# A decoder step on one core: page numbers read later, the first norm's squares added by VectorE, a longer burst of products of ones

## The chip, the cores and the metric

The kernel runs on one core of a Trainium2 chip. The metric is the device time of one execution in microseconds. Shown are the median of three runs and one profiled execution. TensorE multiplies, VectorE and ScalarE prepare and evacuate operands, GpSimd does small side work, and SP (SyncE) issues nearly all loads. ScalarE's queue issues three of them.

## What is computed

One inference step of a two-layer decoder for 256 prompt rows and 8 sample rows (264 columns in all, T), model width 1024. The part that the change touches is the start of layer 0:

```python
def moba_gmlp_mixer(x, pos, past_kv, norm_g, w_in, ...):
    h = rmsnorm(x, norm_g)                       # mean of squares over 1024 features, per row
    z = h @ w_in                                 # 1024 x 2560
    q, k, v, bu, bv = split(z)
    q, k = rope_partial(q, pos), rope_partial(k, pos)
    k_all, v_all = cached pages (page_table) + new k, v   # sample rows only
    a = moba_attention(q, k_all, v_all, pos)     # 8 heads
    b = spatial_gating(gelu(bu), layer_norm(gelu(bv)))
    return x + concat(a, b) @ w_out
```

A ConvFFN (width 2816), a second layer with stick-breaking attention and a pooling mixer, another ConvFFN and a final norm follow. Each of the 8 sample rows has two cached pages of keys and two of values in each layer, found through a page table of 16 numbers.

## The kernel before

Activations lie transposed: features on the 128 partitions, 264 columns in the free dimension, 8 feature tiles. Weights come in blocks of 128x128, in the order in which TensorE uses them. Every fp32 weight block and every operand is split into a high and a low part (`wh`, `wl`; `xg_h`, `xg_l`), ScalarE making the high part and VectorE the low part by a subtraction. Each block then takes three products (high x high, high x low, low x high) of 264 columns each. Eight blocks are one split tile; `wsp` holds four such tiles.

The first norm is applied late: the products of layer 0 use x times the gain, and the factor R (one over the root of the mean square) is multiplied in when a result leaves PSUM. So the squares and the sum for R run beside the first products. `norm0` (line 655) issues the product with a matrix of ones that sums over partitions, then Ln and Exp on ScalarE give R, and three VectorE operations make the rope tables times R. Results that are ready before R (`held`) wait in PSUM.

The first 16 weight blocks arrive with the input in six pieces (`xw`, lines 346 to 352), then come four loads of eight blocks (`raw` 2 to 5, 0.5 MB each) and, from `raw` 6 on, loads of sixteen blocks (1 MB). Calls with `keep_in_program_order` (`late` is one for loads) hold the written order on their engine; the other instructions are ordered by a planner. In the loop `run`, work is hung on block counts: `blk(n, f)` calls f after n of the 160 blocks of layer 0's input projection. TensorE's order is held there (`fixed[0]`), so a product that waits holds all behind it. `page_regs` (line 337) has SP read page numbers from the loaded page table into registers; K and V pages are loaded by `drip_of`, two pages a call. `square` and `sqw` do not exist before; `Norm.add` squares on ScalarE and adds on GpSimd. `WARM` products of ones (128x256, bf16) start TensorE before the first operand is there.

Order of the places that matter: `norm0` at block 30, K pages from block 24 to 80, V pages from 80 to 136, scores S of the prompt from block 82 (`s_qk`), sample scores (`sm_score`) at 131, sample values (`pv_l`, lines 491 to 502) at 157 and 159.

Of the kernel before, what the change touches and what calls it, by code (L numbers as in the profile page):

```python
# [13 lines left out]
AF = mybir.ActivationFunctionType  # L14
ALU = mybir.AluOpType
# [19 lines left out]

MMB = 4
KQ = 5
WARM = 12
YD = ((0, 1), (1, 3), (3, 5), (5, 7), (7, 8))

NEG = -1e30
# [161 lines left out]
def tile_decoder_step(ctx: ExitStack, tc: tile.TileContext, a):  # L203
    nc = tc.nc
    v, s, g = nc.vector, nc.scalar, nc.gpsimd
# [25 lines left out]
    def f4(name, shape=(P, 4, T), dt=F32):  # L231
        return up.tile(list(shape), dt, tag="u", name=name)

    def mv(name):
        return [f4(f"{name}_{x}", dt=F32R) for x in "hl"]
# [4 lines left out]
    def at(name):  # L240
        return psa.tile([P, 512], F32, tag="at", name=name)
# [13 lines left out]
    def vec(n):  # L255
        o, w = _VEC[n]
        return VEC[:, o:o + w]
# [15 lines left out]
    def late(dst, src):  # L273
        tc.keep_in_program_order(nc.sync.dma_start(dst, src))

    def wtiles(tt):
        return [wsp.tile([P, 8 * P], F32R, tag=f"w{x}", name=f"w{x}{tt}") for x in "hl"]

    def raw(ci):
        if ci not in raws:  # L280
            n = _CHUNKS[ci] * P
            r = f4(f"raw{ci}", (P, n)) if ci < C8 else rawp.tile([P, n], F32, tag="raw", name=f"raw{ci}")
            o = (coff[ci] - 16) * P * P
            raws[ci] = r
            late(r, a["w"][o:o + P * n].rearrange("(p f) -> p f", p=P))
        return raws[ci]
# [49 lines left out]
    regs = []  # L336

    def page_regs(n):
        for i in range(len(regs), len(regs) + n):
            regs.append(nc.sync.value_load(PT[0:1, i:i + 1], min_val=0, max_val=NPHYS - 1))  # L340
# [3 lines left out]
    first, o = [], 0  # L344
    for i in range(len(_FIRST)):
        g_, w_, x_ = _first_cols(i)
        n = g_ + w_ + x_
# [4 lines left out]
        if i == 4:  # L352
            raw(2)
    tc.keep_in_program_order(s.dma_start(PT, a["pt"]))
    for c in (3, 4):
        raw(c)
        page_regs(2)
    late(CS, a["rope"].rearrange("p (c t) -> p c t", c=2))
    raw(5)
    page_regs(4)  # L360
    late(CST, a["cst"])
    raw(6)
    page_regs(4)
    late(VEC, a["vec"])
    page_regs(4)
    GAIN = first[0][0]
    xin = [x[:, i, :] for _, _, x in first for i in range(x.shape[1])]
    tc.keep_in_program_order(s.preload_act_table_set("natural_log_exp_and_others"))
# [2 lines left out]
    pw = at("warm")  # L371
    for i in range(WARM):
        tc.keep_in_program_order(pe.matmul(pw[:, :256], warm[:, :P], warm, start=i == 0, stop=i == WARM - 1))

# [9 lines left out]
    def operand_tile(dst, m, src, gain, pin=False):  # L384
        h, l = dst[0][:, m % 4, :], dst[1][:, m % 4, :]
        i = s.activation(h, src, AF.Copy, scale=gain)  # L386
        j = v.scalar_tensor_tensor(l, src, gain, h.bitcast(F32), ALU.mult, ALU.subtract)  # L387
        if pin:
            tc.keep_in_program_order(i)
            tc.keep_in_program_order(j)  # L390

    class Norm:
# [8 lines left out]
        def add(self, m, src=None):  # L401
            q = sm.tile([P, T], F32, tag="sq", name=f"sq_{self.name}{m}")
            i = s.activation(q, X[:, m, :] if src is None else src, AF.Square)
            if src is not None:
                tc.keep_in_program_order(i)
            if m == KD - 1 and self.two:
                self.last.append(q)
            elif self.acc is None:
                self.acc = q
            elif m == (0 if self.seeded else 1):  # L410
                n = sm.tile([P, T], F32, tag="acc", name=f"acc_{self.name}", bufs=2)
                g.tensor_tensor(n, self.acc, q, ALU.add)
                self.acc = n
            else:
                g.tensor_tensor(self.acc, self.acc, q, ALU.add)
# [36 lines left out]
    def page_list(cache, name):  # L452

        tiles, todo = [], []

        def load(i):
            if i % NPG == 0:
                tiles.append(f4(f"{name}_{i}", (P, NPG, 512)))
            late(tiles[i // NPG][:, i % NPG, :], cache[bass.ds(regs[i], 1), :, :].rearrange("o p f -> (o p) f"))

        return tiles, [lambda i=i: load(i) for i in range(NS * NPG)]

    def drip_of(todo, n):
        def f():
            for _ in range(min(n, len(todo))):
                todo.pop(0)()
        return f
# [122 lines left out]
    def residual(gain, name, operand=True, R=None, plain=False):  # L590
        xg = [mv(f"xg_{name}{i}") for i in range(2)] if operand else None
        nrm = Norm(name, not operand)

        def evac(m, o):
            m = m[1]
            if R is not None and not plain:
                z = sm.tile([P, T], F32, tag="rz", name=f"z_{name}{m}", bufs=4)
                v.tensor_tensor(z, o, R, ALU.mult)
                o = z
            v.tensor_tensor(X[:, m, :], X[:, m, :], o, ALU.add)  # L600
            if operand:
                operand_tile(xg[m // 4], m, X[:, m, :], gain[:, m:m + 1])
            nrm.add(m)
            if not operand:
                s.activation(X[:, m, :], X[:, m, :], AF.Copy, scale=gain[:, m:m + 1])
        return xg, nrm, evac
# [7 lines left out]

    xg = [mv(f"xg_0{i}") for i in range(2)]
    nrm = Norm("n0", True)
    for tt in range(2):
        splits[tt] = wtiles(tt)

    def part(i, eng):  # L620

        (b, e), _ = _FIRST[i]
        h, l = [w[:, (b % 8) * P:(b % 8) * P + (e - b) * P] for w in splits[b // 8]]
        src = first[i][1]
        tc.keep_in_program_order(s.activation(h, src, AF.Copy) if eng is s else v.tensor_copy(h, src))
        return lambda: tc.keep_in_program_order(v.tensor_tensor(l, src, h.bitcast(F32), ALU.subtract))

    def whole(tt):
        h, l = splits[tt] = wtiles(tt)
        ci = chunk_of[tt]  # L630
        o = (tt * 8 - coff[ci]) * P
        src = raws[ci][:, o:o + 8 * P]
        tc.keep_in_program_order(s.activation(h, src, AF.Copy))
        tc.keep_in_program_order(v.tensor_tensor(l, src, h.bitcast(F32), ALU.subtract))
# [4 lines left out]
    for m in range(1, 5):  # L639
        part(m, s)()  # L640
        operand_tile(xg[m // 4], m, xin[m], GAIN[:, m:m + 1], pin=True)
        if m != 2:
            nrm.add((m - 1) // 2 if m < 4 else 2, xin[(m - 1) // 2 if m < 4 else 2])
    whole(2)
    for m in range(5, KD):
        operand_tile(xg[m // 4], m, xin[m], GAIN[:, m:m + 1], pin=True)
    for m in range(3, KD):
        nrm.add(m, xin[m])
        if m == 4:
            whole(3)  # L650
        elif m == 6:
            whole(4)
    rope = f4("rope")
    R0, held = [], []

# [43 lines left out]
    ktiles, kload = page_list(a["kt0"], "K0")  # L699
    vtiles, vload = page_list(a["vp0"], "V0")  # L700
# [164 lines left out]
    blk = lambda b, f, *x: hk.at(b / 8 - 1, f, *x)  # L865
# [8 lines left out]
        late(X[:, m:m + 2, :], a["x"].rearrange("p (m t) -> p m t", t=T)[:, m:m + 2, :])  # L874

    for n in range(8):
        blk(24 + 8 * n, drip_of(kload, 2))
        blk(80 + 8 * n, drip_of(vload, 2))
    for m in range(0, KD, 2):
        blk(120 + 4 * m, late_x, m)  # L880
    blk(30, norm0)
    blk(40, masks)
    blk(44, gm_first)
    blk(72, sm_q)
# [39 lines left out]
    xg, nrm, evac = residual(vec("f0"), "f0")  # L924
# [5 lines left out]
    ktiles, kload = page_list(a["kt1"], "K1")  # L930
    vtiles, vload = page_list(a["vp1"], "V1")
# [143 lines left out]
    blk = lambda b, f, *x: hk.at(b / 8 - 1, f, *x)  # L1075
# [28 lines left out]
    xg, nrm, evac = residual(vec("f1"), "f1")  # L1104
# [4 lines left out]
    _, nrm, evac = residual(vec("fin"), "fin", operand=False, R=R, plain=True)  # L1109
# [13 lines left out]
    for i, (m, e) in enumerate(YD):  # L1123
        x = X[:, m:e, :]
# [71 lines left out]
```

## Time and profile before

| | us |
|---|---|
| median of three runs | 602.36 (602.09 to 602.79) |
| the profiled execution | 603.04 |
| its span, first to last instruction | 601.1 |
| TensorE busy | 589.8 (98% of the span) |
| VectorE busy | 425.0 (71%) |
| ScalarE busy | 341.5 (57%) |
| GpSimd busy | 45.5 (8%) |

The profile's page gives busy time and the chain of work that ended last; the views of the trace give, for any stretch, each engine's instructions in order of time, who waited for whom, and the stretch's sums (its start and end, its length, each engine's busy time with the number of instructions, the granted TensorE clock as a share of full speed, the busy share of the load engines and what they moved). "L300" is line 300 of the kernel. PE is TensorE, PEld its weight loads, DVE VectorE, ACT ScalarE, POOL GpSimd, SPq and ACTq the queues that issue loads. Durations of neighbouring instructions on one engine overlap a little, so where a queue is full, the distance from one start to the next is what an instruction costs.

### The profile page before, as it was taken

The page shows a single profiled execution, that of the slowest core. Times are in us where ns is not written, and L with a number is a line of the kernel's source. Part 1 is how long each engine was busy: PE and PEld are TensorE (multiplying, and loading weights), DVE is VectorE, ACT ScalarE, POOL GpSimd, SP SyncE. Part 2 cuts the span into 40 slices and gives each one's busy share as a digit, 9 for nine tenths or more (in the row PEclk, how much of TensorE's full clock was granted, in tenths as well). Part 3 has the DMA queues.
Part 4 walks back from the last instruction along what each step waited for, and adds up shares of the span by engine and source line. Part 5 has one row for each costly group of instructions (what it writes and reads, how often), then busy time and mean ns, then how long its engine had stood idle before and what let it go on. Part 6 is the DMA issues. An engine that isn't in the chain of part 4 may idle for free.

```text
span 601.1 us, 12276 instructions
## 1 busy us (share of the span) xinstructions
PE 589.8 (98%) x4900; PEld 571.1 (95%) x4900; DVE 425.0 (71%) x745; ACT 341.5 (57%) x601; POOL 45.5 (8%) x63
## 2 busy tenths in 40 slices
PE   8999999999999999999999999999999999999994
PEld 7988879999999999999999879999999999999994
DVE  7799665877877778576659676688777787755432
ACT  7657854675555655454453456657565555555441
POOL 4100002400000000001110000130000000002110
PEclk9999999999999999999999999999999999999998
DMA  8998835455454545796467763554645445464502
GB/s 316 355 396 309 294 146 198 156 196 177 174 204 154 203 166 185 261 372 215 154 246 257 270 196 109 172 207 145 210 150 201 177 176 203 152 214 163 189 1 72
DMA packets 28090, 122.39 MB, mean 204 GB/s; under 512 B 3330, under 2 KB 5250, under 8 KB 16642
## 3 DMA queue, kind: packets, MB, share of 16 engines
q1 hardware_dynamic: 27200, 120.42, 56.0%
q10 hardware_dynamic: 834, 1.20, 0.6%
q8 instruction: 38, 0.62, 0.4%
q14 instruction: 18, 0.15, 0.1%
HBM read 117.65 MB, written 3.96 MB: 202 GB/s over the span
## 4 chain that ended last, share of the span: by engine, by line
PE 92%; DVE 3%; DMA 2%; SPq 1%; issue 1%; ACT 0%; ACTq 0%; DVEq 0%
PE mm L215 85%; DMA raw<-in_w 1%; PE pv_l L215 1%; PE sc L215 1%; DVE wl L300 1%; PE pav L215 1%; PE pt L218 1%; DMA PT<-in_pt 1%; PE S L215 1%; SPq L340 1%; PE Z L215 1%; PE pf L215 0%; DVE X L1125 0%; DVE rz_q L689 0%; PE pm L215 0%
## 5 line engine op out<-in xcount | busy, mean ns | idle before, releaser
L300 DVE TENSOR_TENSOR wl<-raw,wh 128x1024 fp32r<-128x1024 f32 x179 | 220.0, 1230 | 113.8 <-ACT wh L299 113.3
L299 ACT ACTIVATE wh<-raw 128x1024 fp32r<-128x1024 f32 x179 | 189.7, 1062 | 193.6 <-PE mm L215 181.6
L215 PE MATMUL mm<-xg_f_h,wh 128*128 128x264 f32 x704 | 200.3, 284 | 0.1
L215 PE MATMUL mm<-xg_f_l,wh 128*128 128x264 f32 x704 | 200.0, 284 | 0.0
L215 PE MATMUL mm<-xg_f_h,wl 128*128 128x264 f32 x704 | 198.6, 282 | 0.0
L215 PEld LDWEIGHTS mm<-xg_f_h,wh 128*128 128x128 f32 x704 | 132.2, 188 | 0.3 <-DVE wk L582 0.3
L215 PEld LDWEIGHTS mm<-xg_f_l,wh 128*128 128x128 f32 x704 | 132.2, 188 | 0.0
L215 PEld LDWEIGHTS mm<-xg_f_h,wl 128*128 128x128 f32 x704 | 132.2, 188 | 0.0
L215 PE MATMUL mm<-a_h,wh 128*128 128x264 f32 x352 | 99.9, 284 | 0.0
L215 PE MATMUL mm<-a_l,wh 128*128 128x264 f32 x352 | 99.8, 284 | 0.0
L215 PE MATMUL mm<-a_h,wl 128*128 128x264 f32 x352 | 99.3, 282 | 0.0
L215 PEld LDWEIGHTS mm<-a_l,wh 128*128 128x128 f32 x352 | 66.1, 188 | 0.0
L215 PEld LDWEIGHTS mm<-a_h,wh 128*128 128x128 f32 x352 | 66.1, 188 | 0.0
L215 PEld LDWEIGHTS mm<-a_h,wl 128*128 128x128 f32 x352 | 66.1, 188 | 0.0
L215 PE MATMUL mm<-xg_h,wh 128*128 128x264 f32 x160 | 48.2, 301 | 0.9 <-ACT xg_h L386 0.9
L215 PE MATMUL mm<-xg_l,wh 128*128 128x264 f32 x160 | 46.2, 289 | 0.0
L215 PE MATMUL mm<-xg_h,wl 128*128 128x264 f32 x160 | 46.1, 288 | 0.1
L215 PE MATMUL mm<-xg_n_h,wh 128*128 128x264 f32 x128 | 38.6, 302 | 0.0
L215 PE MATMUL mm<-xg_n_l,wh 128*128 128x264 f32 x128 | 36.3, 283 | 0.0
L215 PE MATMUL mm<-xg_n_h,wl 128*128 128x264 f32 x128 | 36.2, 283 | 0.0
L215 PEld LDWEIGHTS mm<-xg_h,wh 128*128 128x128 f32 x160 | 30.8, 192 | 4.1 <-issue 2.7
L215 PEld LDWEIGHTS mm<-xg_l,wh 128*128 128x128 f32 x160 | 30.8, 192 | 0.3 <-DVE xg_l L387 0.2
(245 smaller groups left out, 845.3 us busy)
## 6 DMA issues: line engine op xcount, KB each, us to landing
raw<-in_w SPq DMA_DIRECT2D x89, 1024.0 KB, 4.8
K<-in_kt SPq DMA_DIRECT2D x32, 256.0 KB, 6.8
V<-in_vp SPq DMA_DIRECT2D x32, 256.0 KB, 5.5
raw<-in_w SPq DMA_DIRECT2D x4, 512.0 KB, 5.9
X<-in_x SPq DMA_DIRECT2D x4, 264.0 KB, 7.1
xw<-in_xw SPq DMA_DIRECT2D x2, 388.0 KB, 5.2
out_k<-k SPq DMA_DIRECT2D x1, 528.0 KB
out_v<-v SPq DMA_DIRECT2D x1, 528.0 KB, 4.4
```

The lines of the kernel that those rows point to most:

```text
L215: return self.keep(nc.tensor.matmul(*x, **k))
L218: return self.keep(nc.tensor.transpose(*x, **k))
L299: s.activation(h, src, AF.Copy)
L300: v.tensor_tensor(l, src, h.bitcast(F32), ALU.subtract)
L340: regs.append(nc.sync.value_load(PT[0:1, i:i + 1], min_val=0, max_val=NPHYS - 1))
```

## The change

Four things change.

1. SP reads no page number among its first loads; the loads 3 to 6, the rope table, the constants and the vectors are issued one behind the other. Each page number is read when the first K load that needs it is issued.
2. K pages are issued from block 40 to 96 instead of 24 to 80, V pages from block 104 to 146 (every six blocks) instead of 80 to 136 (every eight).
3. The squares of the first norm go to two wide tiles of four feature tiles each. VectorE adds them in three instructions of 1056, 528 and 264 columns, held in order behind its part of split 4. GpSimd adds nothing here any more. The product of ones has one operand instead of two and stands at block 34 instead of 30. The squares of tiles 3 to 7 come behind split 3 on ScalarE.
4. Eighteen products of ones instead of twelve start TensorE.

```diff
-WARM = 12
+WARM = 18
@@
     tc.keep_in_program_order(s.dma_start(PT, a["pt"]))
-    for c in (3, 4):
+    for c in (3, 4, 5):
         raw(c)
-        page_regs(2)
     late(CS, a["rope"].rearrange("p (c t) -> p c t", c=2))
-    raw(5)
-    page_regs(4)
+    raw(6)
     late(CST, a["cst"])
-    raw(6)
-    page_regs(4)
     late(VEC, a["vec"])
-    page_regs(4)
@@
         def load(i):
+            if i >= len(regs):
+                page_regs(1)
             if i % NPG == 0:
@@
     nrm = Norm("n0", True)
+    sqw = [f4(f"sqw{i}") for i in range(2)]
+
+    def square(m):
+        tc.keep_in_program_order(s.activation(sqw[m // 4][:, m % 4, :], xin[m], AF.Square))
+
@@
         operand_tile(xg[m // 4], m, xin[m], GAIN[:, m:m + 1], pin=True)
-        if m != 2:
-            nrm.add((m - 1) // 2 if m < 4 else 2, xin[(m - 1) // 2 if m < 4 else 2])
+        if m < 4:
+            square(m - 1)
     whole(2)
     for m in range(5, KD):
         operand_tile(xg[m // 4], m, xin[m], GAIN[:, m:m + 1], pin=True)
+    whole(3)
     for m in range(3, KD):
-        nrm.add(m, xin[m])
-        if m == 4:
-            whole(3)
-        elif m == 6:
-            whole(4)
+        square(m)
+    whole(4)
+    add = lambda o, x, y: tc.keep_in_program_order(v.tensor_tensor(o, x, y, ALU.add))
+    add(sqw[0], sqw[0], sqw[1])
+    add(sqw[0][:, 0:2, :], sqw[0][:, 0:2, :], sqw[0][:, 2:4, :])
+    add(sqw[0][:, 0, :], sqw[0][:, 0, :], sqw[0][:, 1, :])
+    nrm.acc = sqw[0][:, 0, :]
@@
-        blk(24 + 8 * n, drip_of(kload, 2))
-        blk(80 + 8 * n, drip_of(vload, 2))
+        blk(40 + 8 * n, drip_of(kload, 2))
+        blk(104 + 6 * n, drip_of(vload, 2))
@@
-    blk(30, norm0)
+    blk(34, norm0)
```

## Rows read from the trace of the kernel before

**Rows 1.** The page, part 4: the chain that ended last, by engine.

```profile
PE 92%; DVE 3%; DMA 2%; SPq 1%; issue 1%; ACT 0%; ACTq 0%; DVEq 0%
```

**Rows 2.** Stretches: PE, PEld, DVE, ACT, POOL busy (instructions), clock, load share, GB/s.

```profile
0.00:5.00 5.00, 2.93 (x13) 1.79 (x13) 0.92 (x5) 2.04 (x4) 2.14 (x12) 1.00 0.61 213
4.00:8.60 4.60, 3.79 (x15) 3.50 (x16) 3.78 (x9) 4.12 (x10) 0.22 (x1) 1.00 1.03 416
8.60:18.00 9.40, 9.35 (x77) 9.13 (x76) 9.33 (x10) 7.64 (x15) 5.80 (x6) 1.00 0.96 339
...
23.00:39.40 16.40, 15.23 (x126) 14.90 (x125) 16.37 (x41) 11.60 (x15) 0.00 (x0) 1.00 1.04 403
100.00:200.00 100.00, 100.00 (x828) 100.00 (x827) 78.16 (x132) 61.21 (x108) 7.17 (x8) 1.00 0.51 180
```

**Rows 3.** TensorE's waits, 0 to 60 us: total us, times, longest.

```profile
PE S L215 <- DVE k L695: 1.2, 1, 1.2
```

**Rows 4.** The chain in order of time: start us, us, what.

```profile
1.66 4.86 DMA PT<-in_pt
...
12.93 7.80 DMA raw<-in_w
...
39.41 0.93 PE S L215 x8
```

**Rows 5.** ScalarE in order of time: start, us, line, operation, count, [idle before].

```profile
9.45 1.05 ACT L633 ACTIVATE wh<-raw 128x1024 fp32r<-128x1024 f32 x1
10.40 1.32 ACT L386 ACTIVATE xg_h<-xw,xw 128x264 fp32r<-128x264 f32 x3
11.62 0.73 ACT L403 ACTIVATE sq_n<-xw 128x264 f32<-128x264 f32 x2
...
20.83 1.06 ACT L299 ACTIVATE wh<-raw 128x1024 fp32r<-128x1024 f32 x1 [4.02 <-DMA raw<-in_w]
21.80 0.46 ACT L438 ACTIVATE R_n<-ns_n,epst 128x264 f32<-128x264 f32 x1
22.29 0.42 ACT L439 ACTIVATE R_n<-R_n 128x264 f32<-128x264 f32 x1
```

**Rows 6.** VectorE in order of time, with GpSimd's first add.

```profile
6.68 0.69 DVE L626 TENSOR_TENSOR wl<-xw,wh 128x512 fp32r<-128x512 f32 x1 [0.33 <-ACT wh L625]
...
8.38 1.02 POOL L412 TENSOR_TENSOR acc_n<-sq_n,sq_n 128x264 f32<-128x264 f32 x1 [5.71 <-ACT sq_n L403]
...
8.86 1.09 DVE L626 TENSOR_TENSOR wl<-xw,wh 128x512 fp32r<-128x512 f32 x1
...
21.93 1.22 DVE L300 TENSOR_TENSOR wl<-raw,wh 128x1024 fp32r<-128x1024 f32 x1 [3.18 <-ACT wh L299]
23.07 0.43 DVE L659 TENSOR_TENSOR rope<-ropecs,R_n 128x264 f32<-128x264 f32 x1
...
55.91 1.24 DVE L824 TENSOR_TENSOR bv<-bv,mu 128x1056 f32<-128x1056 f32 x1
```

**Rows 7.** TensorE's products in order of time.

```profile
1.20 2.74 PE L215 MATMUL warm<-warm 128*128 128x256 bf16 x12 [1.20 <-DVE warm L370]
4.81 0.59 PE L215 MATMUL mm<-xg_h,wh 128*128 128x264 f32 x1 [0.87 <-ACT xg_h L386]
...
8.48 0.32 PE L215 MATMUL mm<-xg_h,wl 128*128 128x264 f32 x1
...
18.04 0.61 PE L215 MATMUL ns_n<-acc_n,ones 128*128 128x264 f32 x2
18.48 0.61 PE L215 MATMUL ns_n<-sq_n,ones 128*128 128x264 f32 x2
```

**Rows 8.** The page table: who touches it, duration min/median/max ns, first and last start.

```profile
L340 SPq TENSOR_LOAD <-PT x16: 261/263/473, 6.5 to 17.7; - x16
```

**Rows 9.** Layer 0's V pages: products and loads, the same columns.

```profile
L215 PE MATMUL pv_l<-V,PZ x32: 592/592/617, 83.0 to 87.1; 128*32 128x512 f32 x32
L274 SPq DMA_DIRECT2D V<-in_vp x16: 332/333/1282, 36.7 to 70.1; - x16
```

## The prediction

> **What bounds the kernel now.** I read the page's chain of waits first: 92% of it is TensorE, with small shares for VectorE and loads [rows 1]. So the question is where TensorE is not at its steady pace. The table of stretches answers it [rows 2]: from 100 to 200 us it is busy without a gap and starts 828 products, 0.1208 us each, granted clock 1.00. The final norm and the output behind the last products aren't touched by the change. What is left are the first 40 us. There the list of TensorE's waits has one item inside the stream: 1.2 us before the attention scores S, for key operand k, from VectorE [rows 3]. The stretch from 23.0 to 39.4 us shows why: VectorE is busy for 16.37 of 16.40 us while TensorE does 15.23 [rows 2]. VectorE is the bound there, and its start sets the time of S.
>
> The chain in order of time says what sets that start [rows 4]: the page table lands at 6.52 (1.66 + 4.86); SP reads page numbers between its loads; weight load 6, the first of 1 MB, is issued at 12.93 and takes 7.80. ScalarE then shows the damage [rows 5]: its split (line 299) of that load's first half stands idle for 4.02 us until 20.83, and behind it, on the same queue, waits the Ln of the first norm (21.80, then Exp at 22.29), though the product of ones that feeds it had begun at 18.04 [rows 7]. VectorE waits with it: 3.18 us of idle time before 21.93, and the first rope operation only at 23.07 [rows 6]. S starts at 39.41 [rows 4]; after it TensorE has no wait worth naming until the tail.
>
> **The change part by part.** Times are those of the profiled execution (603.04 us, of which the span is 601.1; the median of the runs shown is 602.36). A gain at S moves all behind it, and I subtract it from the median.
>
> *Page reads and loads.* The 16 reads of page numbers leave their places between loads 3 and 7 and go, one each, in front of the first layer's K pages. At 0.26 us for the read's own instruction [rows 8] 8 reads were at least 2.1 us of SP time in front of load 6, and all of them waited for the page table. Now only loads stand in front of load 6. When does it land? By bytes: the xw pieces (2.13 MB), loads 2 to 5 (2.10), the rope table (0.27) and load 6 itself (1.05) are 5.55 MB. At the rates of the stretches, 213 GB/s to 5 us, 416 to 8.6 and 339 behind [rows 2], 1.07 + 1.50 MB are in by 8.6 and the last 2.98 take 8.8: 17.4, an upper value, because SP's holes are in the 339. ScalarE can split it until 18.4 and its second half until 19.4, and stands free for Ln then. Who pays: each K page costs SP one more read, and the raw loads queue behind them; SP has 2.9 us (24 products) for each two pages, which is enough. K's last pages go from block 80 to 96, 35 blocks or 12.7 us of products ahead of the scoring at block 131. V's last pages go from block 136 to 146; now the last are issued at 70.1, and the V products run from 83.0 to 87.1 [rows 9]; ten blocks are 3.6 us more, and what stands between them. I cost both at nothing; if that cover failed, TensorE would stand at those products.
>
> The Trainium skill (DMA: Bandwidth & Descriptors, Issuing engines are not separate DMA queues) speaks against a gain from issuing early: whatever queue starts them, loads run on the same 16 engines and interleave, and only the issue time is saved. By it load 6 would profit by SP's 2.1 us alone and land at 18.6, its second split would end at 20.6, and the gain below would be some 0.6 smaller (part of the first rival). The trace leans the other way: the engines moved 416 GB/s in one stretch and 339 in the next [rows 2], so there were holes to fill.
>
> *Squares and sum.* ScalarE's order from 9.45 is: split 2, three operands (10.40 to 11.62, so 0.41 each), then squares and splits [rows 5]. By these rows a split costs 0.95 and a square 0.32 to the next start. Changed: split 2 from 9.45, operands from 10.40, split 3 from 11.62, five squares from 12.57, split 4 from 14.2 to 15.2. VectorE finishes its part of split 4 by 16.4 (1.13 to the next start). Then three adds, each reading the one before, so with their whole durations: 1056 columns 1.24, the 528 one by 512 columns 0.69, 264 columns 0.43 [rows 6], 2.36 together: the sum is ready at 18.7. Before, GpSimd added them, and VectorE was slower beside it: the same 512-column subtraction takes 0.69 alone and 1.09 beside GpSimd's add [rows 6]; I have used the undisturbed values. For a 1024-column split that disturbance would be about 0.6, and the sum later by as much.
>
> *The norm.* Its product moves from block 30 to block 34 and is one instead of two; one takes 0.44 us (18.04 to 18.48) [rows 7]. From the sum at 18.7: the product's result after 0.61 [rows 7], Exp 0.49 later, rope 0.78 behind Exp's start [rows 5, 6]: 20.7. Meanwhile VectorE isn't idle: split 5 (1.13) from 18.7 and split 6 from 19.84 to 20.97, and then rope. In the trace split 6 started at 21.93 [rows 6]. From here to k the queue holds the same operations without a gap, so **VectorE is 2.1 us earlier** at S: 37.3 instead of 39.4.
>
> *Products of ones.* Twelve take 2.74 us from 1.20, at 256 columns each the 1.2 GHz level; eighteen need about 4.1, to 5.3. The first real product starts at 4.81 now, so it may lose up to 0.5. From the first to the fifteenth real one (4.81 to 8.48) a product takes 0.26, near the lower level's 0.22 for 264 columns; from there to 18.04 the 76 steps take 0.126, the 2.4 GHz level [rows 7]. The granted clock reads 1.00 in that stretch all the same [rows 2], so I go by the pace. At the steady pace 14 steps would need 1.7 instead of 3.67: 2.0 at most. Bounds -0.5 to +2.0; I take +1.0, by the nearest row: the fifteenth product needs the low part of the third piece of weights, which VectorE ends at 7.37 (6.68 + 0.69) [rows 6] and not sooner afterwards, so that product gains from 8.48 to some 7.4.
>
> The Trainium skill (TensorE: Matmul & The Clock Gate, part 1) speaks against counting on it: the number of slow products at a kernel's start differs from run to run (6, 11 or 14 for one kernel). By it the fifteen are one draw, and the burst may bring 0 or all; the sum below hardly cares.
>
> *Does TensorE arrive in time?* Product 91 was due at 18.04; with +1.0 and twelve more products (1.45) the norm is due at 18.5, waits for the sum until 18.75, and ends at 19.2. The 144 products to block 82 take 17.4 and the mask's two 0.36: it arrives at S at 37.0 and waits 0.3. With no gain from the burst it arrives at 37.7, with -0.5 at 38.2. So the end is set by VectorE, and the burst is worth at most 0.4 to it.
>
> **Sum.** 39.4 - 37.3 = 2.1 us: 602.36 - 2.1 = 600.3 us (profiled execution 600.9, span 599.0). What is late next is still VectorE's k, by 0.3.
>
> **The rivals.**
> *Sum in the wrong place:* split 5 is not held in written order, so it can slip in front of the adds; or VectorE's splits stay as slow as beside GpSimd, or load 6 keeps ScalarE from Ln for a microsecond. With the first the sum is ready at 19.8, the norm ends at 20.3, rope starts at 21.8 instead of 23.07 and the gain is 1.3; with one of the others on top 0.8. For: split 5 is ready at about the same time as the adds. Against: the adds stand before it in the program. 601.1 to 601.6.
> *TensorE decides:* VectorE gets further ahead than I think (adds at less than their whole durations) and TensorE's arrival at 37.0, or 36.3 without a wait for the sum, is the end: gain 2.4 to 3.1, 599.3 to 599.9.
> *The burst does not do what it says:* the pace rises as late as now and the burst only postpones: arrival 37.7 to 38.2, gain 1.2 to 1.7, 600.7 to 601.2.
> *Slower, the sum as a plug:* the norm's product is held in its place in TensorE's order, and all stands behind it. If split 6 slips in front of the adds and load 6 lands as late as now, the adds start at 23.1 and end at 25.5; TensorE stands from 18.5, goes on at 26, and arrives at S at 43.8: 4.4 us slower, 606.8. It decides as soon as the sum comes after 21.2. Against: load 6 can't be that late if SP doesn't read page numbers in front of it.
>
> **How the numbers follow.** Forecast 0.60; TensorE decides 0.08; burst only postpones 0.08; sum late (601.1 to 601.6) 0.16; slower (the plug, or late V pages) 0.08. A measurement of this kernel can tell some 0.2%, 1.2 us, from no change: faster is below 601.2, slower above 603.6. Forecast and TensorE's case are faster, nearly all of the third, a part of the fourth: 0.71; same 0.21; slower 0.08. The range takes all but the slower case and the outermost of the late sum: 599.3 to 601.9.
>
> **What would show it.** Right: ScalarE's split of load 6 without a wait for a load; Ln within half a microsecond of the ones product; no GpSimd adds before 20 us; VectorE without its 3.18 us hole; S near 37.3 with a short wait for k left. Wrong: a wait of TensorE before the norm's product longer than 0.5 us; a rope start after 22 us; a wait at the scoring or at V's products for a load; splits of 512 columns still at 1.09.

## The result: 0.54% slower

| | before | after |
|---|---|---|
| median, us | 602.56 (602.09 to 602.79, 4 runs) | 606.48 (605.08 to 607.42, 4 runs) |
| ratio | | 1.0054 [1.0034, 1.0073] |
| profiled execution, us | 603.04 | 605.08 |
| its span, us | 601.1 | 603.0 |
| first score product on k, us | 39.41 | 40.52 |

The forecast was 600.3 us, 2 us faster than before; the change is 4 us slower, outside the range. The profiled execution of the changed kernel is the fastest of its four, so its trace shows about half of the loss. The rest is in experiment 1. One execution each of experiments 9 (1491 us) and 10 (2046 us), and one of the kernel before beside experiments 11 and 12 (644 us), stand far off the others and are left out of the times and ratios below.

The page's chain by engine, which answers to [rows 1], and the stretches that answer to [rows 2], with one for the new hole from 18 to 22 us:

```profile
PE 94%; DVE 2%; ACT 1%; issue 1%; DMA 1%; DVEq 0%; SPq 0%; ACTq 0%
```

```profile
0.00:5.00 5.00, 3.80 (x19) 2.58 (x19) 0.76 (x5) 1.88 (x3) 2.13 (x12) 1.00 0.60 209
4.00:8.60 4.60, 4.60 (x27) 3.89 (x26) 3.47 (x8) 3.96 (x10) 0.00 (x0) 1.00 1.03 415
8.60:18.00 9.40, 9.40 (x80) 9.40 (x79) 7.88 (x12) 8.95 (x17) 0.00 (x0) 1.00 1.04 419
18.00:22.00 4.00, 0.60 (x5) 0.39 (x4) 4.00 (x5) 0.85 (x1) 0.00 (x0) 1.00 1.00 389
23.00:39.40 16.40, 16.40 (x138) 16.40 (x137) 14.98 (x37) 10.81 (x15) 0.00 (x0) 1.00 0.82 295
```

Up to 18 us all goes as hoped: TensorE is busy without a gap from the burst on, 27 starts against 15 in the second stretch, and the loads move 419 GB/s where they moved 339. Then TensorE stands: 0.60 us of work between 18 and 22, while VectorE is busy for all 4.00. Behind that the roles are exchanged: TensorE is full (16.40 of 16.40) and VectorE has slack (14.98).

TensorE's list of waits names the place (total us, times, longest), where [rows 3] had k:

```profile
PE ns_n L215 <- DVE sqw L653: 3.6, 1, 3.6
PE warm L215 <- DVE warm L365: 1.2, 1, 1.2
PE pmu L215 <- DVE bsum L811: 0.7, 1, 0.7
```

VectorE in order of time shows why the sum is late (answers to [rows 6]):

```profile
15.38 1.23 DVE L636 TENSOR_TENSOR wl<-raw,wh 128x1024 fp32r<-128x1024 f32 x1 [1.11 <-ACT wh L635]
16.52 1.25 DVE L653 TENSOR_TENSOR sqw<-sqw,sqw 128x1056 f32<-128x1056 f32 x1
17.69 2.35 DVE L300 TENSOR_TENSOR wl<-raw,wh 128x1024 fp32r<-128x1024 f32 x2
19.96 0.70 DVE L653 TENSOR_TENSOR sqw<-sqw 128x528 f32<-128x528 f32 x1
20.58 1.22 DVE L300 TENSOR_TENSOR wl<-raw,wh 128x1024 fp32r<-128x1024 f32 x1
21.71 0.43 DVE L653 TENSOR_TENSOR sqw<-sqw 128x264 f32<-128x264 f32 x1
23.91 0.44 DVE L664 TENSOR_TENSOR rope<-ropecs,R_n 128x264 f32<-128x264 f32 x1 [1.77 <-ACT R_n L434]
```

The three adds (line 653) keep their order among themselves, but three splits stand between them: 5 and 6 behind the first add, 7 behind the second. The sum is ready at 22.1, not 18.7. TensorE holds the norm's product in its place and everything behind it with it, so it stands for 3.6 us.

ScalarE, answering to [rows 5]: load 6 no longer keeps it (0.45 us of idle time instead of 4.02, start 16.75 instead of 20.83), but Ln now waits for the product of ones and comes at 22.95, later than the 21.80 of before.

```profile
14.30 1.04 ACT L635 ACTIVATE wh<-raw 128x1024 fp32r<-128x1024 f32 x1
...
16.75 2.10 ACT L299 ACTIVATE wh<-raw 128x1024 fp32r<-128x1024 f32 x2 [0.45 <-DMA raw<-in_w]
22.95 0.48 ACT L433 ACTIVATE R_n<-ns_n,epst 128x264 f32<-128x264 f32 x1 [4.09 <-PE ns_n L215]
```

TensorE's products, answering to [rows 7]: the burst ends at 5.2, five products run at the slow pace, and from 6.66 the starts are 0.12 apart (before: from 8.48).

```profile
1.20 4.02 PE L215 MATMUL warm<-warm 128*128 128x256 bf16 x18 [1.20 <-DVE warm L365]
4.97 0.59 PE L215 MATMUL mm<-xg_h,wh 128*128 128x264 f32 x1
...
6.66 0.31 PE L215 MATMUL mm<-xg_h,wl 128*128 128x264 f32 x1
...
22.20 0.71 PE L215 MATMUL ns_n<-sqw,ones 128*128 128x264 f32 x2 [3.60 <-DVE sqw L653]
...
54.82 0.71 PE L215 MATMUL pmu<-bsum,ones 128*128 128x264 f32 x2 [0.69 <-DVE bsum L811]
```

Two of the prediction's signs of being wrong are there: a wait of 3.6 us before the norm's product, and rope at 23.91. In this execution S is 1.1 us later, and `pmu` (the product of ones over the value operand's sum in `gm_mean`, block 100; the expectations call it the MLP's first sum) stands at 54.82 instead of 52.96, 1.9 later: the span's 1.9.

### The profile page after: what moved, and what is told of

Read it like the earlier page. It is cut to its first block, busy times and chain, and to the rows that moved or that the text cites. A ratio compares the mean times of both kernels' runs of the same rounds, so it can differ in the third digit from the quotient of the medians.

```text
span 603.0 us, 12272 instructions
## 1 busy us (share of the span) xinstructions
PE 589.5 (98%) x4904; PEld 570.8 (95%) x4904; DVE 424.6 (70%) x748; ACT 341.9 (57%) x601; POOL 39.2 (7%) x57
## 4 chain that ended last, share of the span: by engine, by line
PE 94%; DVE 2%; ACT 1%; issue 1%; DMA 1%; DVEq 0%; SPq 0%; ACTq 0%
PE mm L215 86%; PE pv_l L215 1%; PE sc L215 1%; PE pav L215 1%; DMA xw<-in_xw 1%; PE pt L218 1%; PE Z L215 1%; PE S L215 1%; DVE wl L300 0%; ACT sqw L617 0%; PE pf L215 0%; DVE X L1130 0%; ACT wh L635 0%; PE pm L215 0%; PE vtp_v L218 0%
```

## The experiments

My theory after the result had three parts: the splits between the adds stop TensorE; behind that stop the clock falls, which the one profile happens not to show; and the loads by themselves are worth what the forecast said. The rivals were that page reads, later pages or the longer burst cost something, or that the late sum costs through VectorE's k and the stop through nothing. Experiments 1 to 4 ran on one chip with before at 602.92 us, 5 to 8 with 603.0, 9 and 10 with 602.81, 11 and 12 with 602.75; the ratios are to these.

**1. The change again, unaltered.** 

> The changed kernel, unaltered, to see an execution of the common length. Four executions gave 605.1, 606.5, 606.5 and 607.4 us, with mean clocks of 0.995, 0.993, 0.993 and 0.991. Theory C (the hole of 3.6 us before the norm's product lets TensorE's clock fall in most executions): in an execution of 606 us or more the products behind the hole, from 22 us on, start 0.22 us apart instead of 0.12 for some 3 us, and all behind is later by about 1.4; in one of 605 they start 0.12 apart. Rival: the extra 1.4 us lie elsewhere (page loads, tail), and the products behind the hole keep 0.12.

606.60 us (606.39 to 607.64), ratio 1.007 [1.0053, 1.0087]. This trace is one of the slower kind. Two stretches, and the chain behind the hole:

```profile
20.00:25.00 5.00, 2.79 (x11) 2.58 (x12) 2.83 (x6) 1.51 (x5) 0.00 (x0) 0.74 0.79 285
22.00:26.00 4.00, 3.79 (x16) 3.58 (x17) 1.83 (x6) 1.51 (x5) 0.00 (x0) 0.57 0.76 248
```

```profile
22.21 1.10 PE ns_n L215 x2
23.31 18.62 PE mm L215 x144
```

The same stretch of the chain in the first profile:

```profile
22.20 0.71 PE ns_n L215 x2
22.91 17.45 PE mm L215 x144
```

The hole is the same (3.66 us), but the granted clock is 0.57 from 22 to 26 us, and the products from 23.33 to 25.75 start 0.22 us apart, the 1.2 GHz level. The 144 products up to S take 18.62 us here, 17.45 in the first profile at clock 1.00; the norm's product itself takes 1.10 instead of 0.71. Together that is 1.6 us, the difference of the two spans (604.6 and 603.0). So the 3.5 us of this span over before's have three parts: 1.1 at S from the stop, 0.75 between S and `pmu` (experiments 4, 6 and 11 show where from), and 1.6 from the clock. Of the eight executions of this kernel in these two sets one, the first profile, is at a mean granted clock of 0.995 and 605.1; the other seven are at 0.991 to 0.993 and 606.4 to 607.6. Of these seven only this one was traced; that the clock falls at the same place in the other six is a conclusion from their means.

**2. Splits 5 to 7 kept behind the adds.** The change, with VectorE's part of these splits held in the written order:

```diff
-            v.tensor_tensor(l, src, h.bitcast(F32), ALU.subtract)
+            i = v.tensor_tensor(l, src, h.bitcast(F32), ALU.subtract)
+            if tt < 8:
+                tc.keep_in_program_order(i)
```

> Changed kernel, VectorE's part of the splits 5, 6 and 7 also held in written order, so that the three adds stand together behind split 4; nothing else. Theory O (three splits that slipped between the adds hold the sum until 22.1): the sum is there at 18.9, TensorE stands about 0.5 us before the norm's product, rope starts near 21, S near 37.4, and the execution takes 600.5 to 601.3 us. Rival W (VectorE's adds are too slow on this path wherever they stand) or P (the later page loads cost): the hole or another wait stays, 604 us or more.

604.18 us (603.62 to 605.41), ratio 1.003 [1.002, 1.004]: 2.4 us of the loss gone. The adds run from 16.44 to 18.9, and TensorE's wait for them is 0.25 us, as in the forecast's sum. But S starts at 39.1. VectorE in front of k's last add:

```profile
36.85 0.45 DVE L696 STREAM_SHUFFLE rz_k<-mm 128x264 f32<-128x264 f32 x1
37.20 0.41 DVE L700 TENSOR_TENSOR k<-mm,rope 128x264 f32<-128x264 f32 x1
37.53 1.21 DVE L300 TENSOR_TENSOR wl<-raw,wh 128x1024 fp32r<-128x1024 f32 x1
38.66 0.42 DVE L702 TENSOR_TENSOR k<-k,rz_k 128x264 f32<-128x264 f32 x1
```

```profile
PE S L215 <- DVE k L702: 1.8, 1, 1.8
```

The planner has put the next k tile's shuffle and multiply and one more split there, 1.8 us in all, the same as TensorE's wait. (Before has a split in that place too, but not the next k's operations.) And rope starts at 22.23, not near 21, since split 7 stands in front of it. That another order would have k earlier is what experiment 5 tests. Four of the ten executions are at 605.1 to 605.4 with a mean clock of 0.994 against 0.997; none of them was traced, and where the clock fell in them stays open.

**3. Twelve products of ones in the changed kernel.** `WARM = 12`. 

> Changed kernel with 12 products of ones instead of 18. Theory O: the sum still comes at 22.1, so the scores S start as before at about 40.4; TensorE only arrives later at the norm (20 instead of 18.4) and its hole shrinks to about 2 us; profiled execution about 605. Theory C adds: with the shorter hole the clock does not fall, so the executions scatter little, 604.8 to 605.5, below the changed kernel's median of 606.5. Rival (the burst itself costs, by a later first product): 603 or less.

606.64 us (606.54 to 607.61), ratio 1.0066 [1.0049, 1.0083], as with eighteen. The expected shorter hole didn't appear (3.68 us): in this execution no product after the twelve took as long as 0.40 us, where 14 did in before, so TensorE reached the norm no later. One trace with twelve was too narrow a base for the expectation. What the burst does could not be read from this run; experiments 7 and 10 do that.

**4. The loads alone.** The kernel before, with the page reads and the later K and V pages of the change, and neither the squares nor the burst. 

> The kernel before with the page reads and the K and V places of the change, and nothing else (GpSimd adds, norm at block 30, 12 products of ones). By my sum for loads: ScalarE's split of load 6 does not wait 4 us, Ln follows the norm's product at once, rope starts at 20 to 21 instead of 23.1, VectorE's hole of 3.2 us is gone and so is the wait of 1.2 us before S: 600.9 to 601.8 us. Theory P (later pages or reads cost something): no gain, or slower, with a wait at the sample scores or the V products.

602.62 us (602.31 to 603.04), ratio 0.9998 [0.9988, 1.0007]. Load 6 is split at 16.66, Ln starts at 19.21, rope at 20.18, k is ready at 37.4, and S starts on k at 38.23 without a wait, 1.2 us earlier. No product of the V pages waits. Yet the time is that of before. The list of TensorE's waits has a new entry, and VectorE and GpSimd show what is in front of it:

```profile
PE pmu L215 <- DVE bsum L803: 0.6, 1, 0.6
```

```profile
50.70 1.38 DVE L725 TENSOR_SCALAR p<-p,st 128x128 f32<-128x128 f32 x2
52.00 0.42 DVE L803 TENSOR_TENSOR bsum<-bsum,bv 128x264 f32<-128x264 f32 x1
...
50.52 1.27 POOL L797 TENSOR_TENSOR sguc<-sguc,tril 128x512 f32<-128x512 f32 x1 [33.91 <-DVE tril L796]
```

Two multiplies of 128x128 (`p`), 0.48 us in before, take 1.38 beside GpSimd's multiply on the gates' rows (`sguc`). In before that multiply started at 52.43, and a split behind `bsum` paid for it (2.30 us instead of 1.22).

**5. VectorE's order held as far as k.** Experiment 2 with splits up to tile 13 and the q and first k operations held. 

> The whole change, with VectorE's splits of tiles 5 to 13 and its q and first k operations (shuffle, multiplies, add) held in the written order, so that nothing later gets in front of the adds or of k's last add. Theory (what was lost at S is lost to VectorE's order, first at the adds, then in front of k): sum at 18.9, no hole before the norm's product, k ready at 37.0 to 37.4, TensorE's wait for k 0.3 us or less, S at 37.3, that is 1.8 us before the run in which only splits 5 to 7 were held. Rival (VectorE simply has this much to do before k): k again at 39, wait 1.8. Of the 1.8, 0.6 to 1.2 come back at the MLP's first sum, where TensorE waited 0.7 us already; so 602.4 to 603.5 by the theory, 604.2 by the rival.

602.94 us (602.59 to 603.06), ratio 0.9998 [0.9988, 1.0008]. By the medians another 1.2 us of the loss is gone. By the traces it is 0.7: S is at 38.47 instead of 39.14 (not at 37.3), the span 601.0 instead of 601.6. So the order in front of k was worth some 0.7; the rest goes with the four later executions of experiment 2, which no trace shows. An order written by hand has holes of its own: VectorE stood 0.48 us for TensorE's next k products, whose shuffle is written ahead of the first k's last add. At `pmu` the 0.7 us stay.

**6. The gates' rows later.** Experiment 4 with `sgu_load` at block 112 instead of 96. 

> The page reads and cache loads of the change on the kernel before, and the load of the gates' rows (sguc) moved from block 96 to 112, so that GpSimd's multiply on it no longer runs beside VectorE's two softmax multiplies in front of the last add of bsum. Theory (loads alone win 1.3 us at S, and TensorE gives 0.6 to 0.7 of it back waiting for bsum, made late by the VectorE pair slowed beside GpSimd, 1.38 instead of 0.48 us): no wait at the MLP's first products, these at 51.8, span 600.0 to 600.2, time 601.6 to 602.0. Rival (VectorE's own amount of work sets bsum): the wait stays at 0.6, time 602.6.

601.80 us (601.62 to 601.96), ratio 0.998 [0.997, 0.999], 0.8 under experiment 4. The wait is gone and `pmu` starts at 51.76 instead of 52.48. VectorE in the same place:

```profile
50.02 0.47 DVE L725 TENSOR_SCALAR p<-p,st 128x128 f32<-128x128 f32 x2
50.50 0.19 DVE L753 TENSOR_TENSOR own<-q,k 64x32 f32<-64x32 f32 x1
50.72 0.43 DVE L803 TENSOR_TENSOR bsum<-bsum,bv 128x264 f32<-128x264 f32 x1
```

The last add starts 1.28 us earlier; 0.91 of it are the multiplies, the rest mostly two short `tril` operations of VectorE that moved away with the load. The Trainium skill (SBUF — State Buffer, Who interferes with whom) says that VectorE's multiply of one tensor by a scalar can contend with GpSimd for a pair of ports that they share, and that whoever starts first blocks the other. The trace of experiment 4 agrees: GpSimd started first (50.52 against 50.70), and VectorE's pair took 1.38 instead of 0.47 us.

**7. The burst on experiment 6.** `WARM = 18`. 

> The run before this one in the table (loads, gates' rows at block 112) with 18 instead of 12 products of ones and the old sum. Theory (with the old sum TensorE arrives at S without a wait for k, so it is TensorE's start that sets S): S at 37.2 to 37.5 where k's last add allows it, up to 0.7 us earlier than with 12, time 600.8 to 601.4. Rival (the burst brings nothing, since the slow products at the start are a matter of the single run): within 0.2 us of the run with 12.

601.85 us (601.62 to 603.13), ratio 0.9985 [0.9975, 0.9995]: no difference, the rival. (The traced execution, 603.13, has the same span as that of experiment 6, 600.0; its extra 1.3 us lie outside the span.) Seven products take 0.40 us or more at the start, instead of twelve, but the norm's product starts at 18.14 in this trace and at 18.11 in that of experiment 6. With the old sum, VectorE's splits beside GpSimd hold TensorE before 18 us (0.6 us of waits for `wl` here, 0.2 there), and what the burst won is gone.

**8. Order and gates' rows together.** Experiment 5 with `sgu_load` at block 112. 

> The whole change with both repairs: VectorE's order held up to k, and the gates' rows loaded at block 112. Theory (the slip in front of the adds, the slip in front of k and GpSimd beside the softmax multiplies together are all that keeps the change from its forecast): S at 37.3, no wait at the MLP's first products, span 599.0 to 599.6, time 600.6 to 601.2. Rival (another wait turns up behind them): above 602.

602.11 us (601.99 to 602.82), ratio 0.9986 [0.9976, 0.9996]: a miss by 1 us. S at 38.28 behind a 0.9 us wait for k; `pmu` no longer waits. Two repairs make the change a gain, but less than experiment 6 gives without the change's sum.

**9. The adds ahead of split 4.** The change, with the adds where VectorE stands idle for 1.11 us in the profile after, splits 5 and 6 held, and the gates' rows at block 112:

```diff
-    whole(4)
     add(sqw[0], sqw[0], sqw[1])
     add(sqw[0][:, 0:2, :], sqw[0][:, 0:2, :], sqw[0][:, 2:4, :])
     add(sqw[0][:, 0, :], sqw[0][:, 0, :], sqw[0][:, 1, :])
+    whole(4)
```

> The whole change with the three adds put ahead of VectorE's part of split 4 (where it stood idle for 1.1 us and the squares are done), splits 5 and 6 held behind them, and the gates' rows loaded at block 112. Theory (the sum fits into VectorE's own hole; the change loses only by where its adds stand): sum at 16.7, no wait of TensorE before the norm's product, rope from 21.1 behind split 7, k ready at 37.0 to 37.4, S there with a wait of 0.5 us at most, no wait at the MLP's first products; span 599.0 to 599.6, time 600.7 to 601.3, that is 0.5 to 1.1 us under the run with the loads and the gates' rows alone. Rival (something else, TensorE's products of tile 4 or another slip in front of k, takes it back): 601.8 or more.

600.82 us, the fastest of all (600.59 to 601.99; the nine spans are 598.7 to 599.1), ratio 0.9966 [0.9952, 0.9981]. VectorE at the sum, and all that TensorE waits for:

```profile
14.42 1.26 DVE L654 TENSOR_TENSOR sqw<-sqw,sqw 128x1056 f32<-128x1056 f32 x1 [0.16 <-ACT sqw L619]
15.71 1.18 DVE L654 TENSOR_TENSOR sqw<-sqw 128x528 f32<-128x528 f32 x2
16.80 1.22 DVE L638 TENSOR_TENSOR wl<-raw,wh 128x1024 fp32r<-128x1024 f32 x1
```

```profile
PE warm L215 <- DVE warm L367: 1.2, 1, 1.2
PE ns_fin L215 <- ACT sq_fin L400: 0.6, 1, 0.6
PE S L215 <- DVE k L702: 0.2, 1, 0.2
```

The sum is ready at 16.9, the norm's product runs at 18.68 without a wait, S starts at 37.21 and waits 0.25 us for k: the forecast's figures at S, 2.2 us ahead of before, though not by its path (sum at 18.7, rope at 20.97 there; 16.9 and 21.35 here).

**10. Experiment 9 with twelve products of ones.** 

> The run before this one with 12 instead of 18 products of ones. Theory (the burst gives nothing that can be measured, because the number of slow products at the start differs by run with either, and VectorE's k sets S): within 0.3 us of the run with 18. Rival (now that nothing else stands in TensorE's way the burst counts): 0.5 to 1.0 us more than with 18, with S later by as much and no wait for k.

601.71 us (601.21 to 602.25), ratio 0.9981 [0.9971, 0.9991]: the rival again, the burst is worth 0.9 us here. The norm's product starts at 19.55 instead of 18.68, S at 38.09 instead of 37.21; k is late by as much, since its products come later, and the wait for it stays 0.2. VectorE waits for TensorE on the way there:

```profile
28.20 0.01 DVE L696 LOAD_MASK_SELECT rz_q<-mm  x1 [0.86 <-PE mm L215]
```

**11. Experiment 9 without moving the gates' rows.** 

> The whole change with the three adds ahead of split 4 and splits 5 and 6 held behind them; the gates' rows stay at block 96. Theory (the place of the adds alone decides between the change's loss and a gain; the gates' rows are a second, smaller cost): k and S at 37.0 to 37.4 as with the gates' rows later, then a wait of 0.5 to 0.8 us at the MLP's first products; 601.3 to 601.9. Rival (the gates' rows don't matter when VectorE is ahead): no wait there, 600.7 to 601.1.

601.63 us (601.50 to 602.76), ratio 0.9986 [0.9976, 0.9995]. S at 37.24, then 0.7 us of waiting at `pmu`, as by the theory. So the place of the adds alone (and of two splits behind them) is worth some 5 us between this and the change, and moving the gates' rows 0.8 more.

**12. The norm's product ten blocks later.** The change, with `norm0` at block 44; the sum stays late. 

> The change as it is, with the norm's product at block 44 instead of 34, thirty products later; the sum comes as late as in the change, about 22.1. Theory (a product held in its place stops TensorE until the sum is there, and the clock falls behind that hole): the product is due at about 22, so no wait there, granted clock 1.00 from 20 to 28 us; instead TensorE waits 2 to 2.6 us at its 48th tile of products (about 23.6) for an accumulation bank that the value operands still hold until rope's rows are ready; S at 39.5 to 40.0; 602.8 to 604.0 with little scatter if the clock survives the shorter hole. Rival (the loss is the late sum itself, through VectorE's k, and the hole costs nothing): S at 40.5 as in the change, 605 to 606.

603.03 us (602.84 to 603.27), ratio 1.0004 [0.9994, 1.0013]. TensorE:

```profile
22.07 0.71 PE L215 MATMUL ns_n<-sqw,ones 128*128 128x264 f32 x2
25.40 0.36 PE L215 MATMUL mm<-xg_h,wh 128*128 128x264 f32 x1 [1.18 <-DVE bv L702]
```

The sum's last add still starts at 21.59, but thirty products now lie in front of the norm's; it starts at 22.07 without a wait. TensorE then waits 1.18 us for an accumulation bank, the granted clock reads 1.00 from 20 to 28 us, and S starts at 38.46. This one line takes 3.5 us off the change: they went with the product that waited in a held place and with the clock behind it. The late sum is not free either: against experiment 11, which has it early, 1.4 us are left, 1.2 of them at S.

## Why the prediction was wrong, point by point

*Read rightly.* The loads: by bytes and rates load 6 was to be ready at 17.4; its split starts at 16.75. The Trainium skill (DMA: Bandwidth & Descriptors, Issuing engines are not separate DMA queues) says that loads started by several engines interleave on the same 16 engines and that only the time of starting them is saved; the prediction's estimate by it was 18.6. The 419 GB/s of the stretch against 339 before differ from that estimate: holes between the loads got filled. The later pages cost nothing, as costed: no wait at the V products in any run. GpSimd's disturbance ended with its adds: the wide adds took 1.25, 0.70 and 0.43 us (1.24, 0.69 and 0.43 were taken), and a split 1.14 to the next start (1.13). ScalarE's split 4 began at 14.30 (14.2). The norm was due at 18.5; TensorE had its products done at 18.6.

*The burst* was sized at +1.0 us, and the one pair of traces that can show it has 0.87 at the norm's product (experiments 9 and 10). In experiment 3, with twelve, there was nothing to gain: TensorE's products were done at 18.45. First products of 0.40 us or more are 0 to 7 in the nine traces with eighteen ones, and 12 to 18 in four of the five with twelve, with none in the fifth. The fifteenth product starts at 7.47 to 7.95 with eighteen, and at 8.41 to 8.73 in those four; "some 7.4" was the forecast. The Trainium skill (TensorE: Matmul & The Clock Gate, part 1) says that the number of slow ones differs from run to run; both sets agree, and here the longer burst lowers the upper end, from 18 to 7. The step that failed is its use: "worth at most 0.4 to it", since VectorE was to set S. Experiment 10 shows 0.88 at S: k's own products come from TensorE, so a faster TensorE also makes k earlier. VectorE's queue and TensorE's stream are not two independent arrivals.

*The step that failed first* is "then three adds, each reading the one before, so with their whole durations". Their durations were right, their neighbours were not. The adds are held in order among themselves; that keeps nothing else out, and splits 5, 6 and 7 (2.27 us in the one gap, 1.13 in the other) went between. The first rival named one split that "can slip in front of the adds" and priced the sum 1.1 us later for it. Three slipped, and the sum came 3.4 later.

*The slower rival* had the mechanism: "the sum as a plug", the norm's product in its held place, deciding "as soon as the sum comes after 21.2". The sum came at 22.1. Two things in it were wrong. Its condition was tied to a late load 6 ("Against: load 6 can't be that late"): with an early load, whose splits had their high parts by 18.85, the planner put them in front all the same (its reasons are not shown). And its price lacked the clock: S on k came 1.1 us later than before in the first profile and 2.7 later (42.10) in the second, where the clock fell. It got a chance of 0.08, shared with late V pages.

*"From here to k the queue holds the same operations without a gap"* failed next (experiment 2): the operations were others. Split 7 stood in front of rope as well (1.14 us), and two operations of the next k in front of k's last add (0.68); of the 2.1 us of lead 0.27 were left there (38.66 instead of before's 38.93). Held by hand the order gained 0.7 us, with a hole of 0.5 left (experiment 5). Subtracting VectorE's lead at rope from its time at k assumes an order that a planner makes anew for each kernel.

*"After S TensorE has no wait worth naming until the tail"* was the third. It is right for the kernel before, but a list of waits shows no slack, and at `pmu` there was hardly any. Before's last add and TensorE's weight load, and the same load in experiment 6:

```profile
52.28 0.43 DVE L806 TENSOR_TENSOR bsum<-bsum,bv 128x264 f32<-128x264 f32 x1
52.96 0.30 PEld L215 LDWEIGHTS pmu<-bsum,ones 128*128 128x128 f32 x2 [0.33 <-DVE bsum L806]
...
51.76 0.30 PEld L215 LDWEIGHTS pmu<-bsum,ones 128*128 128x128 f32 x2 [0.33 <-issue]
```

The add ended 0.25 us before `pmu` started; where TensorE does wait for it (the profile after) that distance is 0.06, so `bsum` had some 0.2 us to spare. The idle 0.33 us of the weight load, put down to `bsum`, cost nothing: they are there in experiments 6, 8 and 9 without it, and from S to `pmu` it is 13.55 us in before and in experiment 9 alike. A gain at S beyond 0.2 us runs into `bsum` unless VectorE's sum gains as much. In experiment 4 it gained 0.3 where S gained 1.2, and 0.7 us went there.

Put together: with the adds in VectorE's own hole and the gates' rows out of the way (experiment 9) S is at 37.21 with a wait of 0.25, where 37.3 and 0.3 were forecast, and the span is 599.0. So the forecast's end belongs to a kernel three small edits away from the one that was made (adds ahead of split 4, splits 5 and 6 held, the gates' rows later). That the figures agree this closely is in part luck, since the sum came 1.8 us earlier and rope 0.4 later than in the forecast's working.

## What to carry to other kernels

A held instruction fixes its order only against other held ones: for each result that a held product waits for, list every instruction that is ready by then on the producing engine and not held, and price all of them in front of it. Put such a result into a hole that its engine already has, not at the place where its inputs happen to stand in the code; or give the waiting product a place behind the latest time of the result (experiments 9 and 12 are two ways out of the same stop). And before a gain is carried to the end, look for the slack of the results behind it, not only for waits: how long before its use was each one ready?

## What the runs showed of the hardware

That a stop of 3.6 us would cost more than itself was not in the forecast: in seven of eight executions of the change the mean granted clock is lower (0.991 to 0.993 instead of 0.995), and in the one of them that was traced it fell behind the stop: 0.57 from 22 to 26 us, with products 0.22 us apart until 25.75. In experiment 3 the granted clock from 22 to 26 us was 0.50, and the 144 products to S took 19.55 us instead of 17.45. In one execution with the same stop, the first profile, it read 1.00 from 18 us on and the pace never changed. The stops of 1.18 us in experiment 12 and of 1.79 us in experiment 2, and the shorter ones elsewhere, left it at 1.00 in the traces. What decides in which executions it falls was not tried.
